# Moving the chunk operators of a state-space layer to VectorE in short steps, pairing the attention heads, and resizing the weight buffers

## The chip, the cores and the metric

The kernel runs on one core of a Trainium2 chip. The metric is the time of one execution in microseconds (us) on the device. A core has five engines that run their own instruction streams in order and wait for one another through semaphores: TensorE (PE in the rows; its weight loads are PEld), VectorE (DVE), ScalarE (ACT), GpSimd (POOL) and SyncE (SP), which here issues nearly all transfers.

## The reference

Two decoder layers over 256 positions of 1024 channels, all in float32. Each layer runs three token mixers on the same input, sums them through gates, projects, and ends with a feed-forward block:

```
for l in range(2):
    z_sgu, z_ssm, q, k, v, gates = split(x @ w_in[l])        # 6144 columns
    br_a = u * (tril(w_s) @ layer_norm(gelu(v_)) + b_s)      # spatial gating
    h[s] = lam_bar * h[s-1] + b_bar @ z_ssm[s]               # complex state, 32 groups x 64
    br_b = glu(gelu(real(c @ h) + d * z_ssm))
    br_c = causal softmax attention, 8 heads of 64, ALiBi    # one block at this length
    merged = sum of sigmoid(gate) * (branch @ w_branch)
    x = layer_norm(alpha * x + merged @ w_out)
    x = layer_norm(alpha * x + (silu(x @ w1) * (x @ w3)) @ w2)
```

## The kernel before, in words

**Weights.** All weights of both layers come as 272 pieces of 128x1024 floats (512 KB), 136 a layer, in the order in which TensorE uses them (`PLAN`). A piece is loaded by SP into one of `RAW` = 4 raw buffers. ScalarE then copies it, rounded, to `whi` (line 103) and VectorE writes the rest, `wlo = raw - whi` (line 104). `whi` and `wlo` have `NSP` = 6 buffers each; a piece's buffers come free when TensorE has finished with it. Every product with weights is three matmuls (hi x hi, hi x lo, lo x hi), recorded by one helper, line 332. The split of piece i+4 is written into the program just ahead of the matmuls of piece i (`LOOK` = 4), and the load of a piece stands behind the split that frees its raw buffer. So VectorE must get through one `wlo` a piece, whatever else it does.

**Order.** `Flow` counts pieces: its position goes up by one with each piece. Code hands it functions with a due position (`at`, `after`), and they are written into the program at the first tick at or past it. That fixes the order on each engine; what runs when is left to the semaphores. Positions below count from the layer's start, if nothing else is said.

**Chunk operators.** The state-space layer works on chunks of 8 positions and needs, for each layer, operators built from its parameters by `ssm_prep`: tables of powers (`tables`, lines 525 to 571), `bbar` (552 to 556), eight `b_chunk` (`bct`, six 128x256 operations each, lines 577 to 581, then four 128x128 transposes on TensorE, `btp`, line 600, and a copy to `bch`), four `c_chunk` (`cchr`, `cchi`, six 128x512 operations each, the same lines 577 to 581), and the response `kch` (line 621): 16 groups of four small products, 16 and 112 columns wide, for two parts. It goes through DRAM (`kd`) and comes back as eight loads into `tch`. For layer 0 this runs inside the layer's own mixers, for layer 1 inside the feed-forward block of layer 0. `b_chunk` and `bbar` run on GpSimd; `c_chunk` runs on VectorE for layer 0 and on GpSimd for layer 1. `bct` has two buffers, so a chunk waits for the transposes of the second last one. The operators are used by `s_in` (`psi`), `y_own` and `y_past` (`pyc`), which begin at position 32 in layer 0 and 16.5 in layer 1 (`SSM_AT`).

**Attention.** For each head, at a step of 1.85 pieces: `att_s` (scores, `pss`, two matmuls over 64 partitions), `att_max` and `att_norm` (VectorE and ScalarE), `att_t` (three transposes, `ppt`) and `att_v` (`pvy`, two matmuls, 64 columns of output partitions). Two heads share one column block of `qT` and `kT`, one in partitions 0 to 63, the other in 64 to 127.

## Time and profile before

| | us |
|---|---|
| three runs, median (lowest to highest) | 921.89 (918.61 to 924.88) |
| the profiled execution | 922.41 |
| its span, first to last instruction | 920.7 |
| TensorE busy in the span | 874.4 |
| VectorE / ScalarE / GpSimd busy | 601.7 / 423.3 / 202.0 |

The profile is of one execution. Matmuls are pipelined, so that one lasts longer than the time to the next; a busy TensorE is therefore not one at its peak, and what a stretch costs is best seen by laying it beside the same stretch of the other layer. The two layers run the same matmuls with weights; what differs is the work around them. The product `pu` opens the second group of weight pieces; it starts at 20.5 us in layer 0 and at 504.3 us in layer 1. The long run of `p` matmuls that ends the first half of the feed-forward block starts at 284.4 and 735.3 us, and its last `f` matmul ends at 483.3 and 909.6 us. These six times cut the span into stretches that can be compared.

### The profile page before, as it was taken

What the parts mean: (1) busy time and instruction counts of PE and PEld (TensorE: products, weight loads), DVE (VectorE), ACT (ScalarE), POOL (GpSimd) and SP (SyncE); (2) the same over time, 40 slices, a digit from 0 to 9 for tenths busy, and PEclk for the clock granted to TensorE, in tenths of its full rate; (3) what the DMA queues carried; (4) which work ended last, traced back from release to release, by engine and by line L of the source; (5) the groups of instructions that cost most, each with busy time, mean ns of one, the idle gap of its engine ahead of it and who ended that gap; (6) DMA issues with size and microseconds to landing.
All of it is one profiled execution on the core that took longest, in us unless ns stands there. A gap on an engine that the chain in (4) does not pass through costs nothing.

```text
span 920.7 us, 14381 instructions
## 1 busy us (share of the span) xinstructions
PE 874.4 (95%) x5665; PEld 751.2 (82%) x5665; DVE 601.7 (65%) x837; ACT 423.3 (46%) x602; POOL 202.0 (22%) x214
## 2 busy tenths in 40 slices
PE   8978899999999989999988999999999999999996
PEld 7877677778878979998976888777888799999995
DVE  7999955755776586677457477545556766555555
ACT  5535355464544425452324463656454254444440
POOL 2349720011200146799000020000112100000002
PEclk9979899999999999999998999999999999999998
DMA  7563347375455717555865664543846466555531
GB/s 284 198 179 120 115 141 173 111 254 186 164 209 177 274 63 255 164 164 179 157 181 172 220 211 130 161 149 126 268 147 226 159 233 221 187 184 186 191 127 46
DMA packets 52803, 163.26 MB, mean 177 GB/s; under 512 B 6240, under 2 KB 11872, under 8 KB 52704
## 3 DMA queue, kind: packets, MB, share of 16 engines
q1 hardware_dynamic: 52592, 162.09, 55.0%
q8 instruction: 44, 0.72, 0.3%
q10 hardware_dynamic: 144, 0.26, 0.1%
q14 instruction: 23, 0.19, 0.1%
HBM read 157.61 MB, written 4.72 MB: 176 GB/s over the span
## 4 chain that ended last, share of the span: by engine, by line
PE 67%; DVE 12%; POOL 8%; issue 6%; DMA 4%; ACT 3%; SPq 0%; POOLq 0%; DVEq 0%; ACTq 0%
PE pw L332 18%; PE pg L332 13%; PE f L332 9%; PE pb L332 5%; DVE wlo L104 4%; DMA raw<-in_wts_dram 3%; PE p L332 3%; PE pbb L332 2%; PE pkq L332 2%; PE po L332 2%; ACT whi L103 2%; PE pv L332 1%; PE pglu L332 1%; POOL tm L580 1%; PE pa L332 1%
## 5 line engine op out<-in xcount | busy, mean ns | idle before, releaser
L104 DVE TENSOR_TENSOR wlo<-raw,whi 128x1024 fp32r<-128x1024 f32 (+1 forms) x273 | 349.7, 1291 | 233.0 <-ACT whi L103 230.5
L103 ACT ACTIVATE whi<-raw 128x1024 fp32r<-128x1024 f32 (+1 forms) x273 | 284.7, 1053 | 218.1 <-PE pw L332 66.8
L332 PE MATMUL pw<-xT,whi 128*128 128x256 f32 x1152 | 207.8, 284 | 0.0
L332 PEld LDWEIGHTS pw<-xT,whi 128*128 128x128 f32 x1152 | 179.9, 191 | 1.6 <-issue 0.2
L332 PE MATMUL pw<-xT,wlo 128*128 128x256 f32 x576 | 163.4, 284 | 4.5 <-DVE wlo L104 4.3
L332 PE MATMUL pg<-whi,xT 128*128 128x512 f32 x384 | 124.8, 407 | 4.3 <-DVE sgm L936 4.3
L332 PEld LDWEIGHTS pw<-xT,wlo 128*128 128x128 f32 x576 | 111.8, 194 | 4.9 <-DVE wlo L104 4.9
L332 PEld LDWEIGHTS pg<-whi,xT 128*128 128x128 f32 x384 | 70.2, 191 | 22.2 <-DVE sgm L936 4.7
L428 POOL TENSOR_SCALAR ve<-mv 128x1 f32<-128x1 f32 x12 | 6.7, 561 | 338.6 <-DVE mv L426 338.5
L1058 POOL TENSOR_TENSOR mg<-mg,tg 128x512 f32<-128x512 f32 x16 | 23.6, 1482 | 248.1 <-DVE tg L1056 248.0
L332 PE MATMUL pg<-wlo,xT 128*128 128x512 f32 x192 | 76.2, 397 | 0.0
L332 PE MATMUL f<-whi,hch 128*128 128x512 f32 x144 | 57.9, 402 | 2.0 <-ACT hch L499 2.0
L332 PE MATMUL f<-whi,hcl 128*128 128x512 f32 x144 | 57.9, 402 | 0.8 <-DVE hcl L500 0.8
L332 PE MATMUL f<-wlo,hch 128*128 128x512 f32 x144 | 56.8, 394 | 0.0
L332 PE MATMUL pkq<-xT,whi 128*128 128x256 f32 x256 | 47.2, 287 | 0.0
L332 PE MATMUL p<-whi,xT 128*128 128x512 f32 x128 | 40.8, 397 | 3.2 <-DVE xT L195 3.2
L332 PEld LDWEIGHTS pg<-wlo,xT 128*128 128x128 f32 x192 | 36.6, 191 | 8.4
L332 PEld LDWEIGHTS pkq<-xT,whi 128*128 128x128 f32 x256 | 39.7, 192 | 1.2 <-issue 1.2
L332 PE MATMUL po<-whi,xT 128*128 128x512 f32 x128 | 40.2, 395 | 0.0
L332 PE MATMUL pkq<-xT,wlo 128*128 128x256 f32 x128 | 36.0, 282 | 0.0
L332 PEld LDWEIGHTS f<-whi,hch 128*128 128x128 f32 x144 | 27.5, 191 | 8.1 <-ACT hch L499 2.4
L332 PEld LDWEIGHTS f<-wlo,hch 128*128 128x128 f32 x144 | 28.0, 194 | 6.4
(265 smaller groups left out, 1522.9 us busy)
## 6 DMA issues: line engine op xcount, KB each, us to landing
raw<-in_wts_dram SPq DMA_DIRECT2D x271, 512.0 KB, 4.0
ln<-in_lng_dram SPq DMA_DIRECT2D x8, 512.0 KB, 8.0
xt<-in_xt_dram SPq DMA_DIRECT2D x4, 256.0 KB, 5.5
ud<-ut SPq DMA_DIRECT2D x4, 256.0 KB, 4.7
xch<-ud SPq DMA_DIRECT2D x8, 128.0 KB, 3.7
zd<-zs SPq DMA_DIRECT2D x8, 128.0 KB, 3.8
ztk<-zd SPq DMA_DIRECT2D x4, 256.0 KB, 4.8
xres<-in_x_dram SPq DMA_DIRECT2D x2, 512.0 KB, 6.9
```

The costliest lines, as they stand in the source:

```text
L103: nc.scalar.activation(hi[:, p], t[:, p], AF.Copy)
L104: nc.vector.tensor_tensor(lo[:, p], t[:, p], hi[:, p].bitcast(F32), OP.subtract)
L332: T_.matmul(o, l, r, start=start, stop=stop, skip_group_check=True)
L428: G.tensor_scalar(ve, mv[:, 1:2], eps, None, OP.add)
L580: lambda: (eng.tensor_tensor(tm, x_re, y_im, OP.mult), eng.tensor_tensor(o_im, o_im, tm, OP.subtract if conj else OP.add))]
L1058: G.tensor_tensor(merged[t][:, cc], merged[t][:, cc], tg, OP.add)
```

## The change

The numbers of the plan: `RAW` 4 to 3 (raw buffers), `NSP` 6 to 7 (split buffers), `SSM_AT` (32, 16.5) to (38, 17), `ATT_STEP` 1.85 a head to 3.75 a pair. A table `SHIFT` of 32 entries moves single steps by -1.5 to +2 pieces. `bbar`, `b_chunk` and `c_chunk` all run on VectorE, in both layers; the six operations of a chunk are handed out in three steps of two, a third of the chunk's step apart, where `b_chunk` was one block before; and the frame tables are spread at 1.25 pieces a step. For layer 0, `c_chunk` comes first (from 12.5, every 2.25), then `b_chunk` (from 22, every 1.6; transposes 3 later). For layer 1, counted from the middle of the feed-forward block, `c_chunk` comes from 8 every 3 and `b_chunk` from 22 every 3. The first 16 columns of `cch` hold the scaled `c`, so that the response is one 128-column product for each group and part. The eight loads of `tch` stand 1.5 pieces apart for layer 1 (1.0 before) and begin at 25 (46 before). One addition of the spatial gating's layer norm moves from GpSimd to VectorE, two small scalings go from VectorE to ScalarE, `as` and `at` have two buffers where they had three, and the last products of layer 0's feed-forward block take both halves in turn for the second row tile.

```diff
-SSM_AT = (32.0, 16.5)
-W2_STEP = (3, 2, 2, 2, 2, 2, 2, 2, 1)
-RAW, NSP, LOOK = 4, 6, 4
+SSM_AT = (38.0, 17.0)
+W2_STEP = (3, 2, 2, 2, 2, 2, 2, 1, 2)
+RAW, NSP, LOOK = 3, 7, 4
-ATT_AT, ATT_STEP = 24.5, 1.85
+ATT_AT, ATT_STEP = 24.5, 3.75
+ASB = 2
...
         def b_chunk(c):
...
-            for f in cmul(G, o[0], o[1], x[0], x[1], y[0], y[1], tm, False):
-                f()
-            st["bct", c] = o
+            for n, f in enumerate(cmul(o[0], o[1], x[0], x[1], y[0], y[1], tm, False)):
+                after(db / 3 * n, f)
...
-            for n, f in enumerate(cmul(E, o[0], o[1], x[0], x[1], y[0], y[1], tm, True)):
+            for n, f in enumerate(cmul(o[0], o[1], x[0], x[1], y[0], y[1], tm, True)):
                 after(dc / 3 * n, f)
...
-                    for part in range(2):
-                        r = cch[k][:, n, 0:112] if part else cst[:, k, n, :]
-                        oo = o[:, 16:128] if part else o[:, 0:16]
-                        T_.matmul(oo, st["bb"][:, k, n, :], r, start=j == 0 and k == 0 and part == 0,
-                                  stop=k == 1, skip_group_check=True, tile_position=(0, 32 * g))
+                    T_.matmul(o, st["bb"][:, k, n, :], cch[k][:, n, 0:P], start=j == 0 and k == 0, stop=k == 1,
+                              skip_group_check=True, tile_position=(0, 32 * g))
...
+        at(t0 - 1.5, scale_c, "scc")
+        for n, f in enumerate(tables()):
+            at(t0 + 0.25 * n, f, "lam")
+        for n, f in enumerate(frame()):
+            at(tb + 1.25 * n, f, f"tab{n}")
+        for c in range(4):
+            at(c0 + dc * c, lambda c=c: c_chunk(c), f"cc{c}")
...
+            at(b0 + db * c, lambda c=c: b_chunk(c), f"bc{c}")
+            at(b0 + db * c + lag, lambda c=c: b_transpose(c), f"bt{c}")
...
-    ssm_prep(0, lambda t, f: fl.at(t, f), V, 8.0, 2.25, 4.25, 6.0, 3.0, 0.75)
+    ssm_prep(0, lambda t, f: fl.at(t, f), 10.5, 24.0, 12.5, 2.25, 22.0, 1.6, 3.0, 0.75)
...
+        def att_s(m):
+
+            bs = [bank("pss") for _ in range(2)]
+            for cs, t in ((slice(0, 128), 0), (slice(128, 384), 1)):
+                for o in range(2):
+                    rr = slice(64 * o, 64 * o + 64)
+                    T_.matmul(bs[o][0][:, cs], qT[rr, m, P * t:P * t + P], kT[rr, m, 0:P * (t + 1)], start=True,
+                              stop=True, skip_group_check=True, tile_position=(64 * o, 0))
...
+            for cs, t, c0 in ((slice(0, 256), 0, 0), (slice(256, 384), 1, 128)):
+                for o in range(2):
+                    h = 2 * m + o
+                    T_.matmul(po[64 * o:64 * o + 64, c0:256], vt[t][:, 64 * h:64 * h + 64], at_s[h][:, cs],
+                              start=t == 0, stop=t == 1, skip_group_check=True, tile_position=(0, 64 * o))
...
-            after(6.0, lambda: ssm_prep(l + 1, lambda t, f: fl.at(pos0 + t, f), G, 8.0, 2.75, 5.25, 24.0, 2.5, 1.0))
+            after(2.0, lambda: ssm_prep(l + 1, lambda t, f: fl.at(pos0 + t, f), 6.0, 8.0, 8.0, 3.0, 22.0, 3.0, 4.5, 1.5))
```

How the order moves, at three places. In brackets stand the semaphores that a row waits for, by the engine or transfer queue that raises them. The first is VectorE in layer 0, before the change, ahead of the split of piece 13. Between the splits of pieces 12 and 13 stand 23 operations of the tables in one block, of which these are the last eleven (`tab` and `tm` are the frame tables and their scratch):

```order
L528 TENSOR_TENSOR lam<-lam,tm 128x16x4
L569 COPY tab<-par_c_138 128x16
L569 COPY tab<-par_s_139 128x16
L525 TENSOR_TENSOR tm<-tab 128x32 [waits DVE_49]
L526 TENSOR_TENSOR tab<-tab 128x32
L527 TENSOR_TENSOR tab<-tab,tm 128x16 [waits DVE_49]
L528 TENSOR_TENSOR tab<-tab,tm 128x16
L525 TENSOR_TENSOR tm<-tab 128x64 [waits DVE_49]
L526 TENSOR_TENSOR tab<-tab 128x32x2
L527 TENSOR_TENSOR tab<-tab,tm 128x16x2 [waits DVE_49]
L528 TENSOR_TENSOR tab<-tab,tm 128x16x2
L104 TENSOR_TENSOR wlo_514<-raw_390,whi_513 128x1024 [waits DMAHW5_49,PE_49,Activation_49]
```

With the change the tables stand elsewhere, and a typical place of the busiest stretch of layer 0 on VectorE reads so (`tmb` is the scratch of `b_chunk`, `ISA` the score step of attention, each `wlo` a piece):

```order
L107 TENSOR_TENSOR wlo_1116<-raw_952,whi_1115 128x1024 [waits DMAHW6_49,PE_49,Activation_49]
L584 COPY tab<-par_c_136 128x16
L593 TENSOR_TENSOR bct<-bct,tmb 128x256 [waits DVE_49]
L594 TENSOR_TENSOR bct<-bu,lam 128x256
L107 TENSOR_TENSOR wlo_1147<-raw_998,whi_1146 128x1024 [waits DMAHW7_49,PE_49,Activation_49]
L595 TENSOR_TENSOR tmb<-bu,lam 128x256 [waits DVE_49]
L596 TENSOR_TENSOR bct<-bct,tmb 128x256 [waits DVE_49]
L1003 ISA as,ast<-pss,dist 128x128 [waits PE_49]
L1003 ISA ast 128x1
L1003 ISA as,ast<-pss,dist 128x256
L1003 ISA ast 128x1
L592 TENSOR_TENSOR bct<-bu,lam 128x256 [waits PE_49]
```

What moved: a chunk's six operations stand in twos between the splits, beside the attention's. The last of these rows opens a `b_chunk` and waits for TensorE. The second place is GpSimd before the change, where that wait stood: a whole `b_chunk` of layer 0 and the addition behind it.

```order
L577 TENSOR_TENSOR bct<-bu,lam 128x256 [waits PE_49]
L577 TENSOR_TENSOR tm<-bu,lam 128x256 [waits Activation_49]
L578 TENSOR_TENSOR bct<-bct,tm 128x256 [waits Pool_49]
L579 TENSOR_TENSOR bct<-bu,lam 128x256
L580 TENSOR_TENSOR tm<-bu,lam 128x256 [waits Pool_49]
L581 TENSOR_TENSOR bct<-bct,tm 128x256 [waits Pool_49]
L916 TENSOR_TENSOR vv<-vv,sg_b 128x512 [waits DMAHW3_49,DVE_49]
```

What moved: the six operations and their wait for TensorE went from GpSimd's queue to VectorE's, where the next pieces' `wlo` stand behind them. The third place is TensorE in layer 0 where the scores of a head are made, before the change (`pg`, the gates' products, around them):

```order
L332 MATMUL pg_1170<-whi_982,xT 128x512 x2
L332 MATMUL pg_1170<-wlo_983,xT 128x512
L973 MATMUL pss<-kT,qT 128x128
L974 MATMUL pss<-kT,qT 128x256
L332 MATMUL pg_1182<-whi_982,xT 128x512 x2
L332 MATMUL pg_1182<-wlo_983,xT 128x512
L332 MATMUL pg_1182<-whi_982,xT 128x512 x2
```

and with the change (here the products of a branch, `pb`, stand around them):

```order
L614 MATMUL btp<-ident,bct 128x128 x4
L992 MATMUL pss<-kT,qT 128x128 x2
L992 MATMUL pss<-kT,qT 128x256 x2
L1020 MATMUL ppt<-ident,as 128x128 x3
L340 MATMUL pb_1298<-whi_1115,brah 128x512
L340 MATMUL pb_1298<-whi_1115,bral 128x512
L340 MATMUL pb_1298<-wlo_1116,brah 128x512
```

What moved: two heads' score products stand side by side, as do, later, two heads' `pvy` products (64x256 twice, then 64x128 twice).

## Rows read from the trace of the kernel before

**Rows 1.** The page: busy time, share of the span and instructions of each engine, and the granted clock in 40 slices of the span (9 is full speed).

```profile
PE 874.4 (95%) x5665; PEld 751.2 (82%) x5665; DVE 601.7 (65%) x837; ACT 423.3 (46%) x602; POOL 202.0 (22%) x214
PEclk9979899999999999999998999999999999999998
```

**Rows 2.** Windows: the stretch and its length, then busy time of PE, PEld, DVE, ACT and POOL with instruction counts, granted clock, DMA share and GB/s. The first two rows are layer 0 from `pu` to the feed-forward block, the next two the same in layer 1, then the feed-forward block of layer 0 and of layer 1.

```profile
20.50:140.00 119.50, 103.19 (x688) 89.38 (x687) 102.38 (x190) 55.59 (x92) 62.33 (x66) 0.91 0.48 152
140.00:284.40 144.40, 141.85 (x888) 111.11 (x887) 92.70 (x131) 69.90 (x114) 14.00 (x12) 1.00 0.56 179
504.30:618.00 113.70, 111.84 (x869) 92.51 (x867) 67.84 (x105) 61.89 (x108) 6.12 (x11) 1.00 0.54 175
618.00:735.30 117.30, 114.84 (x547) 92.46 (x546) 72.84 (x91) 56.04 (x82) 14.95 (x12) 1.00 0.56 185
284.40:483.30 198.90, 189.37 (x1348) 174.01 (x1347) 128.87 (x144) 83.09 (x98) 91.75 (x81) 0.97 0.60 182
735.30:909.60 174.30, 174.30 (x1186) 161.22 (x1185) 97.88 (x100) 75.22 (x83) 0.84 (x3) 1.00 0.54 178
```

**Rows 3.** Timeline of TensorE: two neighbouring groups of the response; each group ends with the four records of a `cst` row.

```profile
432.86 0.24 PE L621 MATMUL kch<-cst,bb 128*32 128x16 f32 x4
...
433.15 0.24 PE L621 MATMUL kch<-cst,bb 128*32 128x16 f32 x4
```

**Rows 4.** Groups of TensorE over the whole span: 128-column products on four column groups of 32, and full-array transposes of 128 columns.

```profile
L780 PE MATMUL psi<-bch,uch 128*32 128x128 f32 x128 | 4.5, 276 | 1.9 <-ACT uch L762 1.9
L485 PE MATMUL mtp<-ident,mg 128*128 128x128 f32 x32 | 4.5, 272 | 0.0
```

**Rows 5.** Waits of TensorE: what waited, for what, us in total, times, longest.

```profile
PE psu L332 <- DVE wlo L104: 5.9, 2, 3.5
PE pw L332 <- DVE wlo L104: 4.3, 1, 4.3
PE pg L332 <- DVE sgm L936: 4.3, 1, 4.3
PE btp L600 <- POOL bct L581: 4.1, 2, 2.9
PE kch L621 <- POOL cchi L581: 2.2, 1, 2.2
```

**Rows 6.** Timeline of VectorE in layer 0: start, us, line, operation. Left out between the `wlo` rows are the tables.

```profile
39.95 1.22 DVE L104 TENSOR_TENSOR wlo<-raw,whi 128x1024 fp32r<-128x1024 f32 x1 [1.17 <-ACT whi L103]
...
47.70 1.64 DVE L104 TENSOR_TENSOR wlo<-raw,whi 128x1024 fp32r<-128x1024 f32 x1
...
55.99 3.49 DVE L104 TENSOR_TENSOR wlo<-raw,whi 128x1024 fp32r<-128x1024 f32 x3
```

**Rows 7.** Groups of VectorE from 740 to 900 us (layer 1, feed-forward): busy us, mean ns of one.

```profile
L104 DVE TENSOR_TENSOR wlo<-raw,whi 128x1024 fp32r<-128x1024 f32 x59 | 72.3, 1225 | 65.7 <-ACT whi L103 65.1
```

**Rows 8.** Windows of 20 us in the mixers of layer 0, same columns.

```profile
40.00:60.00 20.00, 14.12 (x81) 13.10 (x80) 19.48 (x43) 6.17 (x8) 8.88 (x12) 0.79 0.55 165
100.00:120.00 20.00, 16.01 (x166) 13.09 (x166) 19.86 (x23) 5.56 (x9) 14.67 (x13) 0.83 0.35 112
```

**Rows 9.** Groups of VectorE from 360 to 437 us (layer 0, feed-forward).

```profile
L104 DVE TENSOR_TENSOR wlo<-raw,whi 128x1024 fp32r<-128x1024 f32 x25 | 42.4, 1711 | 17.4 <-ACT whi L103 17.4
L500 DVE SCALAR_TENSOR_TENSOR hcl<-hh,hch 128x512 fp32r<-128x512 f32 x4 | 5.3, 1328 | 0.0
```

**Rows 10.** Groups of VectorE from 70 to 120 us (layer 0, mixers).

```profile
L104 DVE TENSOR_TENSOR wlo<-raw,whi 128x1024 fp32r<-128x1024 f32 x11 | 18.0, 1633 | 1.6 <-ACT whi L103 1.6
L580 DVE TENSOR_TENSOR tm<-cst,lam 128x512 f32<-128x512 f32 x4 | 4.5, 1129 | 0.0
```

**Rows 11.** Groups of VectorE over the whole span: two-input operations of the two sizes at issue, where GpSimd is idle.

```profile
L812 DVE TENSOR_TENSOR vch<-rot 128x256 f32<-128x256 f32 x4 | 1.7, 426 | 0.1
L455 DVE TENSOR_TENSOR xres<-xres,ln 128x512 f32<-128x512 f32 x2 | 1.3, 680 | 0.0
```

**Rows 12.** Transfers over the whole span: size, median us from issue to landing.

```profile
raw<-in_wts_dram SPq DMA_DIRECT2D x271, 512.0 KB, 4.0
tch<-kd SPq DMA_DIRECT2D x2, 256.0 KB, 7.1
```

**Rows 13.** Transfers from 436 to 490 us (layer 0's `tch` loads for layer 1 and its last pieces).

```profile
raw<-in_wts_dram SPq DMA_DIRECT2D x14, 512.0 KB, 6.7
```

**Rows 14.** Groups of GpSimd over the whole span.

```profile
L579 POOL TENSOR_TENSOR bct<-bu,lam 128x256 f32<-128x256 f32 x16 | 17.7, 1109 | 0.0
L577 POOL TENSOR_TENSOR bct<-bu,lam 128x256 f32<-128x256 f32 x16 | 13.7, 857 | 32.0 <-PE btp L600 19.2 <-DVE lam L527 6.7 <-DVE lam L528 6.1
```

**Rows 15.** Timeline of TensorE in layer 1: the scores of one head up to its first transposes, and the value products of one head.

```profile
588.28 0.48 PE L973 MATMUL pss<-kT,qT 64*128 64x128 f32 x2
588.61 0.59 PE L974 MATMUL pss<-kT,qT 64*128 64x256 f32 x2
589.13 0.55 PE L1000 MATMUL ppt<-ident,as 128*128 128x128 f32 x3
593.77 0.65 PE L1014 MATMUL pvy<-at,vt 128*64 128x256 f32 x2
594.26 0.38 PE L1016 MATMUL pvy<-at,vt 128*64 128x128 f32 x2
```

**Rows 16.** The page: the group of ScalarE that makes `whi`, over the whole span (busy us, mean ns of one, idle time before them and what ended it).

```profile
L103 ACT ACTIVATE whi<-raw 128x1024 fp32r<-128x1024 f32 (+1 forms) x273 | 284.7, 1053 | 218.1 <-PE pw L332 66.8
```

More of the change, by code (lines that the diff above doesn't have):

```diff
@@ L168, in tile_hybrid_trunk @@
     tick, after = fl.tick, fl.after
-    prs = sp.tile([P, 56 * DEPTH], F32, tag="as", name="prs", bufs=3)
+    prs = sp.tile([P, 56 * DEPTH], F32, tag="as", name="prs", bufs=ASB)
     xT = cp.tile([P, 2, KD, S], F32R, name="xT")
@@ L358, in go @@
             if q == npc - 1:
-                after(ev[t] if isinstance(ev, (tuple, list)) else ev, lambda: evac(t, *outs[t]))
+                after((ev[t] if isinstance(ev, (tuple, list)) else ev) + SHIFT.get(f"{fl.layer}e{name}", 0),
+                      lambda: evac(t, *outs[t]))
             if t == 1:
@@ L639, in response_load, with at @@
                               k_dram.rearrange("h (g m) -> h g m", g=8)[:, :, 0:4 * P - 64 * t])
[L641 to L652 removed]
+        def at(t, f, key):
+            put(t + SHIFT.get(str(l) + key, 0), f)
+        at(t0 - 1.5, scale_c, "scc")
[5 more added lines that the diff above has]
+            at(c0 + dc * c, lambda c=c: c_chunk(c), f"cc{c}")
+        for c in range(2):
+            at(c0 + dc * c + 0.5 * dc, lambda c=c: bbar(c), f"bb{c}")
+        for c in range(8):
+            at(b0 + db * c, lambda c=c: b_chunk(c), f"bc{c}")
+            at(b0 + db * c + lag, lambda c=c: b_transpose(c), f"bt{c}")
+        t1 = c0 + 4 * dc + 1.5
+        at(t1, response, "resp")
         for t in range(LC):
[L654 removed]
+            at(t1 + 3.5 + lt * t, lambda t=t: response_load(t), "rl")
     dram = ctx.enter_context(tc.tile_pool(name="dram", bufs=1, space=bass.MemoryType.DRAM))
@@ L668, in tile_hybrid_trunk @@
     bch = cp.tile([P, 16, 2, P], F32, name="bch")
-    cch = [cp.tile([P, 16, P], F32, name="cch" + s) for s in "ri"]
+    cch = [cp.tile([P, 16, P + 16], F32, name="cch" + s) for s in "ri"]
     tch = cp.tile([P, 8, 4 * P], F32, name="tch")
@@ L696, in tile_hybrid_trunk, with at @@
         fl.pos = base
-        def at(t, f):
-            fl.at(base + t, f)
+        fl.layer = l
+        def at(t, f, key=""):
+            fl.at(base + t + SHIFT.get(str(l) + key, 0), f)
         sg = {}
@@ L1239, in tile_hybrid_trunk @@
         for t in range(2):
-            for c in range(2):
-                for n, kk in enumerate(range(done, FFT)):
-                    w2_part(kk, t, c, last[n])
-                    if t == c == 1:
-                        W.finish()
-                    tick(0.25)
-                after(0.25, lambda t=t, c=c: (ln_half(t, c, a2[t, c][0]), a2[t, c][1]()))
+            order = [(c, n) for c in range(2) for n in range(FFT - done)]
+            if t == 1 and not end:
+                order = [(c, n) for n in range(FFT - done) for c in range(2)]
+            for c, n in order:
+                w2_part(done + n, t, c, last[n])
+                if t == c == 1:
+                    W.finish()
+                tick(0.25)
+                if n == FFT - done - 1:
+                    after(0.25, lambda t=t, c=c: (ln_half(t, c, a2[t, c][0]), a2[t, c][1]()))
             after(0.25, lambda t=t: ln_last(t, gb2) if end else ln_fin(t, gb2, keep))
```

194 lines of the change are left out of this document (89 added, 105 removed).

## The prediction

> **What bounds the kernel now.** I read the page first: TensorE is busy for 874.4 of 920.7 us, VectorE for 601.7, and the granted clock drops only here and there [rows 1]. A TensorE that is busy for 95% looks like the end of the matter, but matmuls overlap, so busy time says little. I therefore laid the two layers side by side, since their weight matmuls are the same [rows 2]. From the product `pu` to the same point of the feed-forward block, layer 0 takes 119.5 + 144.4 = 263.9 us and layer 1 takes 113.7 + 117.3 = 231.0: 32.9 more. The rest of the feed-forward block takes 198.9 and 174.3: 24.6 more. These 57.5 us are what the operators of both layers cost, since both are built in layer 0's time, one set in each stretch. TensorE's own share is small: a response is 16 groups of 433.15 - 432.86 = 0.29 us [rows 3], 4.6 us, and 32 transposes at 4.5 / 32 = 0.14 us [rows 4] are 4.5 us at most, together 9.1 in each stretch. So 57.5 - 18.2 = 39.3 us are waits and half clock: about 23.8 in the mixers, 15.5 in the feed-forward block.
>
> The waits name the cause [rows 5]: TensorE waited for `wlo` of VectorE, for `sgm` of VectorE, and for `bct` and `cchi` of GpSimd. Two things make VectorE late. First, blocks: between two splits stands the whole frame table, and the splits begin at 39.95, 47.70 and 55.99 us [rows 6], where a piece goes by in 2.7 us (59 splits in 160 us [rows 7]). In that window TensorE is busy for 14.12 of 20 us and the granted clock averages 0.79 of the full 2.4 GHz, that is, part of it at 1.2 [rows 8]. Second, GpSimd: a split takes 1.225 us where GpSimd is idle [rows 7], 1.711 beside its chunk operators in the feed-forward block [rows 9] and 1.633 in the mixers [rows 10].
>
> **The change, part by part.** The sum is made against the profiled execution, 922.4 us (span 920.7 and 1.7 around it), which stands 0.5 above the median of 921.89.
>
> *Chunk operators on VectorE.* A 128x256 operation with two inputs takes 0.426 us there, a 128x512 one 0.680 [rows 11]. Layer 0's mixers get 48 operations of `b_chunk` and 6 of `bbar` at 0.426, 23.0 us, and 2 additions of 0.68, 1.4: 24.4 in. What leaves: its 24 `c_chunk` operations took about 1.13 beside GpSimd [rows 10] and will take 0.68, 10.8 us; about 20 splits that stood beside GpSimd's 62.3 busy us lose 0.41 each, 8.2 us [rows 2, 7, 10]. That is 24.4 - 19.0 = 5.4 us more for VectorE, which was busy for 102.4 of 119.5 us in the first stretch [rows 2]. So VectorE is not relieved, it is smoothed: TensorE's inputs no longer queue behind a block of 23 operations, and the chunks are spread as far as position 36. If VectorE were busy without a pause, the first stretch could end at 102.4 + 5.4 = 107.8 us, 11.7 earlier. That is the upper bound of this term in the first stretch, 0 is the lower one, and I take 10, since the blocks go for certain. The state-space products move from position 32 to 38, out of the crowded stretch into one in which TensorE was busy for 141.85 of 144.4 us, so they cost there what they save here; I count neither.
>
> In the feed-forward block VectorE gets 24 `c_chunk` operations (16.3 us) and the same 54 smaller ones (23.0), and loses 25 x 0.49 = 12.2 of slow splits and 4 x 0.64 = 2.6 of slow `hcl` (1.328 against a `128x512` operation of 0.68) [rows 7, 9, 11]: 128.9 + 24.5 = 153.4 of 198.9 us [rows 2]. It has room. The waits for GpSimd go, and the loads of `tch` move away from the layer's end, where raw loads took 6.7 us to land instead of 4.0 [rows 12, 13]. Of 15.5 us I take 13; bounds 4 (the wait for `wlo` of 4.3 alone) and 15.5. The cover is 3 to 4 pieces of split weights ahead of TensorE, some 8 to 11 us. If it is gone, each late operation shows in full.
>
> *The wait that moves.* GpSimd waited 19.2 us for TensorE's `btp` ahead of `bct` [rows 14]; that wait now stands on VectorE, with the next splits, evacuations and attention steps behind it. The old wait was long because GpSimd ran ahead. VectorE is as loaded as TensorE and will mostly arrive later. I price it at 0 and keep 9.6 us (half of it, the part that the four pieces ahead may not cover) for the rivals.
>
> *Attention in pairs.* One head's scores last from 588.28 to 589.13, 0.85 us; its value products some 0.73 (0.49 to the second shape's start, and half as much for half the columns) [rows 15]. Sixteen heads: 25.3 us. Two heads side by side use different rows of the array for scores, different columns for values. If they overlap fully, half goes: 12.6 us; if not, 0. The nearest row is `psi`: 128 products on neighbouring column groups are busy for 4.5 us in all, 0.035 each, where full-array passes of the same 128 columns take 0.14 [rows 4]. So neighbours in different groups do overlap, by more than two. I take 10.5 of 12.6, as some of layer 0's attention lies where VectorE, not TensorE, ends last.
>
> A rule speaks against the half of this that uses columns: the Trainium skill, "TensorE: Matmul & The Clock Gate", section "Part 3: Packing small matmuls — row/col tiling", says that a weight load overlaps running matmuls only when its row group differs. The two heads' value products share all rows; by that rule half of their 11.7 us, 5.8, would not go and the sum would be up to 5 us higher, about 893. The `psi` products share all rows too, and 0.035 us each leaves no room for weight loads that stand alone, so this case's trace does not agree.
>
> *Half the response products.* 0.29 us a group holds two 16-column and two 112-column products; without the former I estimate 0.23 (0 to 0.29 as bounds): 32 x 0.06 = 2 us.
>
> *Buffers.* A raw buffer is taken while its load lands and is split: 4.0 + 1.05 (`whi`) + 1.2 = 6.3 us [rows 7, 12, 16]. Three of them give a piece every 2.1 us, against 2.7 needed; four gave 1.6. I price it at 0; where a load takes 6.7 us [rows 13], it is 9.0 / 3 = 3.0, and the pieces ahead must cover the difference, so I give up 1 us for the `tch` loads. The seventh split buffer may help where pieces are held longer, at the layer's seam; no row prices that, so 0.
>
> Sum: 10 + 13 + 10.5 + 2 - 1 = 34.5; 922.4 - 34.5 = 887.9, say **888 us**.
>
> **Rivals.**
> *VectorE inherits the wait.* VectorE arrives at `bct` first, waits for transposes, and the splits behind it come late. For it: both engines are near full in layer 0, the pieces are coupled both ways, and `btp` in turn must find its chunk ready. Against it: VectorE is the busier one. The smoothing in the mixers then brings nothing and the feed-forward block gives up 4: 888 + 10 + 4 = 902; with the whole 9.6 instead, 912.
> *The pairs don't overlap.* Then 10.5 stays: 898. For it: no row shows two 64-row groups beside each other. Against it: `psi`.
> *All waits go.* 23.8 + 15.5 + 12.6 + 2 = 53.9: 868. Against it: VectorE's 107.8 us above.
> *Slower: three raw buffers starve the split.* With three, a load that takes over 3 x 2.7 - 2.3 = 5.8 us makes weights the bound. Transfers of `tch` took 7.1 [rows 12], raw loads beside them 6.7. If raw loads take 8 us for 80 of the 272 pieces, each costs (8 + 2.3) / 3 - 2.7 = 0.73, 59 us: 888 + 59 = 947 less the 10 that the pieces ahead cover, 937. Against it: the median of 4.0 over 271 loads, and three quarters of the span have no `tch` load near.
> *The change doesn't do what it says* on VectorE if short steps still pile up, since a tick hands out all that is due; that is the first rival again.
>
> **How the numbers follow.** The forecast's own case (878 to 897) has 0.49, VectorE's wait 0.20, no overlap 0.13, all waits gone 0.10, starved splits 0.08. About 1% is what a measurement of this kernel tells from no change: 912.7 and 931.1. The first, third and fourth case lie below 912.7, and so does most of the second: 0.49 + 0.13 + 0.10 + 0.09 = 0.81 faster. The rest of the second is 0.11 for the same, 0.08 slower. The range from 867 to 911 leaves out the starved case and the end of the second and fourth.
>
> **What would show it.** In the profile after: splits at 1.23 us everywhere; GpSimd busy well under 100 us; no wait of TensorE for GpSimd; the stretch from `pu` to the feed-forward block some 15 us shorter in layer 0 and 5 in layer 1; the feed-forward block of layer 0 within 15 us of layer 1's; scores and values of a pair in about the time of one head. Wrong would be: VectorE's waits for `btp` or TensorE's for `wlo` over 10 us in all, `pss` and `pvy` as long as before, or ScalarE's `whi` waiting for raw loads ahead of TensorE's waits.

## The result and the profile after

The changed kernel takes 881.29 us (median of four runs, 877.84 to 881.99), the kernel before 922.32 in the same job: a ratio of 0.9551, 95% interval 0.9509 to 0.9592. The forecast of 888 was 6.7 us too high, within its range. The profiled execution after took 881.44 us, its span 879.7. The page, against [rows 1]:

```profile
PE 840.5 (96%) x5537; PEld 727.3 (83%) x5537; DVE 613.2 (70%) x971; ACT 423.5 (48%) x604; POOL 54.2 (6%) x78
PEclk9989989999999999999999999999999999999998
```

GpSimd's busy time fell from 202.0 to 54.2 us, VectorE's rose by only 11.5 although it took over the chunks. The four stretches between the same matmuls as in [rows 2] (from `pu` to the feed-forward block in layer 0 and in layer 1, then the two feed-forward blocks; start, end and length, busy PE, PEld, DVE, ACT and POOL, granted clock, DMA share, GB/s):

```profile
20.40:271.80 251.40, 233.09 (x1511) 191.77 (x1509) 195.06 (x379) 128.03 (x210) 22.74 (x23) 0.97 0.56 176
473.60:695.20 221.60, 218.74 (x1414) 181.46 (x1412) 144.04 (x198) 118.58 (x192) 17.27 (x21) 1.00 0.57 185
271.80:452.90 181.10, 178.83 (x1283) 165.24 (x1283) 140.83 (x221) 84.05 (x99) 1.33 (x2) 1.00 0.70 202
695.20:868.60 173.40, 173.40 (x1185) 161.06 (x1185) 95.31 (x98) 74.34 (x82) 0.79 (x2) 1.00 0.56 182
```

Layer 0's mixers took 263.9 us and take 251.4, layer 1's 231.0 and now 221.6, layer 0's feed-forward block 198.9 and now 181.1, layer 1's 174.3 and now 173.4. The largest part came from the feed-forward block: it stands 7.7 us behind layer 1's, where it stood 24.6 behind (the mark of its last `f` product stands 2.2 us, in layer 1 2.7, ahead of that product's end, in both kernels alike). Layer 0's mixers are still 29.8 behind layer 1's (32.9 before).

A part of this is TensorE's clock. The same windows from layer 0's mark to the next `pu`, before and after:

```profile
284.40:504.30 219.90, 207.59 (x1421) 188.47 (x1420) 146.16 (x165) 91.89 (x109) 93.08 (x83) 0.95 0.59 180
271.80:473.60 201.80, 196.10 (x1357) 178.74 (x1357) 156.87 (x242) 90.82 (x108) 2.70 (x4) 0.99 0.68 198
```

In the trace the time at 1.2 GHz adds up to 20.5 us in the first row and to 3.4 in the second; the rest is at 2.4 GHz. In layer 0's mixers it is 17.1 where it was 20.5. Before, each fall of the clock in this stretch came with a stop of TensorE, of 4.3, 2.2, 2.0 and 2.5 us, or just behind it; after, a stop of 2.3 us for a chunk had none behind it. At the lower level a 512-column product took 0.43 us to the next one, at 2.4 GHz 0.23 (`f` from 475.43 and from 479.14 us), so a wait with a fall behind it costs more than its own length. The 17.1 us less at the lower level are worth at most some 8 of this stretch's 18.1; that is an estimate from these rows.

The groups of VectorE over the whole span that answer to [rows 7, 9, 10, 11] (busy us, mean ns of one, idle time ahead and what ended it):

```profile
L107 DVE TENSOR_TENSOR wlo<-raw,whi 128x1024 fp32r<-128x1024 f32 (+1 forms) x273 | 334.6, 1233 | 182.8 <-ACT whi L106 180.0 <-PE f L340 1.3
L509 DVE SCALAR_TENSOR_TENSOR hcl<-hh,hch 128x512 fp32r<-128x512 f32 x18 | 12.3, 685 | 2.0 <-ACT hch L508 2.0
L592 DVE TENSOR_TENSOR bct<-bu,lam 128x256 f32<-128x256 f32 x16 | 6.7, 419 | 0.0
L595 DVE TENSOR_TENSOR tmc<-cchr,lam 128x512 f32<-128x512 f32 x8 | 5.5, 685 | 0.0
```

A split takes 1.233 us on average over the whole span now, the operations of a chunk 0.42 and 0.68, as the prediction costed them. TensorE's waits, against [rows 5] (total, times, longest):

```profile
PE utp L778 <- ACT xgr L770: 4.6, 1, 4.6
PE btp L614 <- DVE bct L596: 3.9, 3, 2.3
PE ppt L1020 <- ACT bch L615: 3.4, 1, 3.4
PE kch L632 <- DVE cchi L596: 2.1, 1, 2.1
```

The long waits for `wlo` and `sgm`, 14.5 us in all, are gone. The waits for chunks are not: they moved with the chunks to VectorE, 3.9 and 2.1 us where 4.1 and 2.2 stood. New are two waits for ScalarE, 8.0 us: `utp` (transposes of the state-space input, which wait for its reordered copy `xgr`) and `ppt`. Among VectorE's waits no row names `btp` (0.5 us in the second profile, `a_same` below): it did not inherit the 19.2 us that GpSimd had waited [rows 14].

### The profile page after: what moved, and what is told of

Its sections match the earlier page's. It is cut to its first block, busy times and chain, and to the rows that moved or that the text cites. A ratio compares the mean times of both kernels' runs of the same rounds, so it can differ in the third digit from the quotient of the medians.

```text
span 879.7 us, 14083 instructions
## 1 busy us (share of the span) xinstructions
PE 840.5 (96%) x5537; PEld 727.3 (83%) x5537; DVE 613.2 (70%) x971; ACT 423.5 (48%) x604; POOL 54.2 (6%) x78
## 4 chain that ended last, share of the span: by engine, by line
PE 54%; DVE 18%; issue 10%; DMA 9%; ACT 6%; POOL 2%; SPq 1%; POOLq 0%; DVEq 0%; ACTq 0%
PE pw L340 15%; PE pg L340 13%; PE f L340 9%; DMA raw<-in_wts_dram 8%; DVE wlo L107 7%; PE pb L340 4%; ACT whi L106 3%; PE p L340 2%; PE pkq L340 2%; PE pbb L340 2%; PE pglu L340 1%; PE pu L340 1%; DMA ud<-ut 1%; POOL mg L1075 1%; PE pyc L855 1%
## 5 line engine op out<-in xcount | busy, mean ns | idle before, releaser
L107 DVE TENSOR_TENSOR wlo<-raw,whi 128x1024 fp32r<-128x1024 f32 (+1 forms) x273 | 334.6, 1233 | 182.8 <-ACT whi L106 180.0
L106 ACT ACTIVATE whi<-raw 128x1024 fp32r<-128x1024 f32 (+1 forms) x273 | 285.5, 1053 | 230.1 <-DMA raw<-in_wts_dram 153.8
L340 PE MATMUL pw<-xT,whi 128*128 128x256 f32 x1152 | 203.7, 280 | 0.0
L340 PEld LDWEIGHTS pw<-xT,whi 128*128 128x128 f32 x1152 | 176.5, 188 | 1.6 <-issue 0.2
L340 PE MATMUL pw<-xT,wlo 128*128 128x256 f32 x576 | 161.2, 280 | 0.0
L340 PE MATMUL pg<-whi,xT 128*128 128x512 f32 x384 | 122.4, 400 | 0.0
L340 PEld LDWEIGHTS pw<-xT,wlo 128*128 128x128 f32 x576 | 109.8, 191 | 0.1
L340 PE MATMUL f<-whi,hcl 128*128 128x512 f32 x144 | 56.1, 389 | 0.0
L340 PEld LDWEIGHTS f<-whi,hcl 128*128 128x128 f32 x144 | 27.1, 188 | 5.0
```

The lines of the kernel that those rows point to most:

```text
L106: nc.scalar.activation(hi[:, p], t[:, p], AF.Copy)
L107: nc.vector.tensor_tensor(lo[:, p], t[:, p], hi[:, p].bitcast(F32), OP.subtract)
L340: T_.matmul(o, l, r, start=start, stop=stop, skip_group_check=True)
```

## The experiments

Each was timed in five rounds beside the kernel before; since the runs were made in groups on different chips, ratios to it are compared. `a_same` ran in one group with `b_pairs`, `a_block` and `a_raw46`. The stretches are those of the windows above, from each run's own profile; the third reaches here to the next `pu`.

| run | median us | ratio to before (95%) | mixers 0 | mixers 1 | feed-forward 0 to `pu` |
|---|---|---|---|---|---|
| before | | 1 | 263.9 | 231.0 | 219.9 |
| after | 881.29 | 0.9551 (0.9509 to 0.9592) | 251.4 | 221.6 | 201.8 |
| after again, `a_same` | 879.32 | 0.9537 (0.9507 to 0.9568) | 249.9 | 222.1 | 199.7 |
| `b_pairs` | 915.84 | 0.9930 (0.9902 to 0.9957) | 268.0 | 224.9 | 215.9 |
| `b_frame` | 912.04 | 0.9903 (0.9875 to 0.9932) | 261.1 | 230.7 | 214.6 |
| `a_single` | 878.35 | 0.9545 (0.9521 to 0.9569) | 250.2 | 221.8 | 199.9 |
| `a_resp2` | 880.39 | 0.9561 (0.9540 to 0.9582) | 249.3 | 222.5 | 201.9 |
| `a_block` | 885.54 | 0.9596 (0.9568 to 0.9625) | 255.2 | 221.8 | 202.9 |
| `a_bpool0` | 875.29 | 0.9503 (0.9481 to 0.9524) | 247.8 | 221.6 | 199.4 |
| `a_bpool1` | 882.50 | 0.9580 (0.9555 to 0.9605) | 249.9 | 221.5 | 204.8 |
| `a_pool1` | 889.19 | 0.9646 (0.9621 to 0.9671) | 250.2 | 221.8 | 208.3 |
| `a_late` | 884.31 | 0.9606 (0.9580 to 0.9633) | 251.2 | 222.0 | 204.0 |
| `a_raw46` | 878.34 | 0.9521 (0.9492 to 0.9551) | 249.0 | 222.2 | 199.7 |
| `a_best` | 877.10 | 0.9520 (0.9495 to 0.9546) | 248.1 | 221.5 | 200.8 |

**The changed kernel again** (`a_same`), no edit:

> The kernel after, unchanged, to have its time beside the other runs of this group on one chip and to see how far two profiles of the same program differ. Every theory: 878 to 882 us.

It took 879.32 us. Two profiles of this one program differ by 1.5 us in layer 0's mixers and 2.1 in its feed-forward block: that is the grain of the table, and a difference of 2 us in a stretch says nothing yet.

**Attention in pairs alone** (`b_pairs`), on the kernel before; the functions `att_s` and `att_v` and their steps are those of the diff, buffers as before (the load of `x` for the residual moves 1.7 pieces earlier with them):

```diff
-ATT_AT, ATT_STEP = 24.5, 1.85
+ATT_AT, ATT_STEP = 24.5, 3.75
-        def att_s(h):
+        def att_s(m):
...
-        def att_v(h):
+        def att_v(m):
```

> The kernel before, with the attention in pairs of heads alone. Theory of the prediction (two heads' products overlap, and most of TensorE's time in them counts): 10 to 13 us faster, 909 to 912. Rival (in layer 0 the attention lies where VectorE and ScalarE end last, so only layer 1's half counts): 6 us faster, 916, the mixers of layer 1 shorter by 6 and those of layer 0 the same.

The ratio is 0.9930, some 6.5 us. The windows of the two mixers, layer 0 and layer 1:

```profile
20.40:288.40 268.00, 241.32 (x1575) 199.35 (x1574) 195.82 (x321) 125.50 (x206) 76.66 (x78) 0.94 0.53 165
504.30:729.20 224.90, 220.74 (x1415) 183.25 (x1414) 140.53 (x195) 117.83 (x191) 21.02 (x23) 0.99 0.58 185
```

Layer 1 gains 6.1 of the 6.3 us that half of 12.6 makes: there the pairs overlap fully and count fully. Layer 0 gains nothing, its mixers are 4.1 longer. That is the rival's side, which had them unchanged: TensorE's time in the attention does not set the end there. The granted clock of that stretch is 0.94, where it was 0.96 [rows 2], that is 30.7 us at 1.2 GHz instead of 20.5, and TensorE has new waits in it (`ppt` 3.8 us, `pg` 3.1). That two heads at once make a longer block for VectorE and ScalarE, and so bring these waits, is my reading. In the feed-forward block another 4.0 went, where this edit changes no instruction; that is twice the grain. It goes with 10.2 us at 1.2 GHz instead of 20.5; why TensorE stopped less there is open. What the pairs do in layer 0 of the changed kernel, where the steps around them differ, no run shows.

**Head after head** (`a_single`), on the changed kernel:

```diff
-            for cs, t in ((slice(0, 128), 0), (slice(128, 384), 1)):
-                for o in range(2):
+            for o in range(2):
+                for cs, t in ((slice(0, 128), 0), (slice(128, 384), 1)):
...
-            for cs, t, c0 in ((slice(0, 256), 0, 0), (slice(256, 384), 1, 128)):
-                for o in range(2):
+            for o in range(2):
+                for cs, t, c0 in ((slice(0, 256), 0, 0), (slice(256, 384), 1, 128)):
```

> The kernel after, with one change: the score and value products of a pair are written head after head (first both of one head, then both of the other) instead of alternately; placement on the array and everything else stay. Theory (products overlap only where neighbours stand in different row or column groups): of four products in a row only the middle two are then neighbours in different groups, so about two thirds of the 12.9 us that TensorE's time for pss and pvy fell by come back, +8 us, about 889. Rival (the gain came from fewer, larger steps and not from the overlap): within 2 us of 881.

No difference. My reason for the forecast of +8 fell, and so did the rival's reason, since the overlap stayed. TensorE's timeline around the scores of a pair, first as changed, then head after head:

```profile
567.57 0.39 PE L340 MATMUL pg<-wlo,xT 128*128 128x512 f32 x1
567.88 0.93 PE L992 MATMUL pss<-kT,qT 64*128 64x128 f32 x8
568.74 0.50 PE L340 MATMUL pg<-whi,xT 128*128 128x512 f32 x1
```

```profile
564.80 0.39 PE L340 MATMUL pg<-wlo,xT 128*128 128x512 f32 x1
565.12 0.93 PE L992 MATMUL pss<-kT,qT 64*128 64x128 f32 x8
565.98 0.50 PE L340 MATMUL pg<-whi,xT 128*128 128x512 f32 x1
```

A pair's scores take 0.86 us to the next product in both, where one head alone took 0.85 [rows 15]. The single records of the scores head after head say how (start in us and columns; each product has two records):

```
565.118  128
565.131  128
565.331  128
565.344  128
565.443  256
565.456  256
565.661  256
565.674  256
```

The order in the kernel's text is 128, 256, 128, 256 columns, and still the two 128-column products start 13 ns apart and both 256-column ones come after them. The second head's first product started ahead of the first head's second; the instructions of the built program were not listed for this run, so whether TensorE or the build changed the order is not shown. Here it was enough that products for different parts of the array stood near each other; they did not have to alternate. The value products of a pair, which differ in columns of the array alone:

```profile
576.52 0.87 PE L1032 MATMUL pvy<-at,vt 128*64 128x256 f32 x8
577.32 0.50 PE L340 MATMUL pb<-whi,brah 128*128 128x512 f32 x1
```

They take 0.80 us for two heads, where one took about 0.73 [rows 15]. The rule of the Trainium skill that spoke against it ("TensorE: Matmul & The Clock Gate", section "Part 3: Packing small matmuls — row/col tiling", a weight load overlaps running products only when its row group differs) does not agree with this trace: these products use all 128 rows, and the saving is nearly as full as for the scores.

**The response in two products again** (`a_resp2`):

```diff
-                    T_.matmul(o, st["bb"][:, k, n, :], cch[k][:, n, 0:P], start=j == 0 and k == 0, stop=k == 1,
-                              skip_group_check=True, tile_position=(0, 32 * g))
+                    for c0, c1 in ((0, 16), (16, P)):
+                        T_.matmul(o[:, c0:c1], st["bb"][:, k, n, :], cch[k][:, n, c0:c1],
+                                  start=j == 0 and k == 0 and c0 == 0, stop=k == 1,
+                                  skip_group_check=True, tile_position=(0, 32 * g))
```

> The kernel after, with one change: each 128-column product of the response is written as a 16-column and a 112-column product again. Theory (a 16-column product costs TensorE as much time as the 36 ns that the records of before show, so that halving the products was worth 5 us and not the 2 of the prediction): +4 to +5.5 us, about 886. Rival (the prediction's size): +2 us, 883.

It took 880.39, ratio 0.9561, within the interval of the unchanged kernel and nearer the rival's 2 us. TensorE's own time for the response did change. In the changed kernel, layer 1's response (16 groups, four to each pair of rows; the first rows and the last, with the product behind):

```profile
346.20 0.45 PE L632 MATMUL kch<-cchr,bb 128*32 128x128 f32 x8
346.44 0.42 PE L632 MATMUL kch<-cchi,bb 128*32 128x128 f32 x8
...
347.75 0.49 PE L632 MATMUL kch<-cchi,bb 128*32 128x128 f32 x8
348.17 0.38 PE L340 MATMUL pw<-xT,whi 128*128 128x256 f32 x1
```

It lasts from 346.20 to 348.17, 0.12 us a group where it was 0.29 [rows 3]. That is 2.7 us a layer, 5.4 in all, more than the 2 of the prediction; but the kernel's time shows at most 2 of it. One reason stands in the traces: layer 0's response lasts 4.90 us in `a_resp2` and still 4.39 in the changed kernel, since the quicker one stops for 2.1 us to wait for `cchi`.

**Chunks in one block** (`a_block`), both kinds, both layers:

```diff
             for n, f in enumerate(cmul(o[0], o[1], x[0], x[1], y[0], y[1], tm, False)):
-                after(db / 3 * n, f)
+                f()
...
             for n, f in enumerate(cmul(o[0], o[1], x[0], x[1], y[0], y[1], tm, True)):
-                after(dc / 3 * n, f)
+                f()
```

> The kernel after, with the six operations of each chunk (b and c, both layers) written as one block at the chunk's first step instead of in three steps. Theory of the prediction (short steps let the splits through, which is what the mixers of layer 0 gain from): 5 to 10 us slower, 884 to 891. Rival (a block of six lasts 2 to 4 us, and the three to four pieces ahead cover it): within 2 us of the unchanged kernel.

It is 6 us slower than `a_same` in the same job (885.54 against 879.32), and the mixers of layer 0 took most of it: 255.2 against 249.9; the feed-forward block took 3.2 more, little above the grain. The short steps are worth about 5 us in layer 0's mixers. The same work on the same engine, in other places between the splits, costs that much.

**Frame tables spread alone** (`b_frame`), on the kernel before:

```diff
-            at(t0 + 0.125 * n if n < 14 else t0 + 3.0 + 0.5 * n, f)
+            at(t0 + 0.125 * n if n < 5 else t0 + 14.0 + 1.25 * (n - 5), f)
...
-            u = tm[:, :n * 2 * k].rearrange("p (c i t) -> p c i t", i=n, c=2)
+            t = work("gq", (P, 512), name="tmt", bufs=3) if tm is None else tm
+            u = t[:, :n * 2 * k].rearrange("p (c i t) -> p c i t", i=n, c=2)
...
-            todo += doubling(V, tabv, tm, 16, NCH)
+            todo += doubling(V, tabv, None, 16, NCH)
```

> The kernel before, with the frame tables alone spread (their eight steps from piece 22 on, 1.25 apart, in place of 0.125 apart from piece 8.6 on). Theory of the prediction (the block of 23 operations between two splits is one of two causes of what layer 0's mixers lose): 4 to 8 us faster, 914 to 918, the wait of psu for wlo gone. Rival (the block is paid later, where VectorE is as full): within 2 us of 922.

912.04 us, ratio 0.9903, 8 to 9 us faster than before and more than the 4 to 8 expected: a fifth of the change by moving eight steps (with a scratch tile for each step in place of one for all). The waits of TensorE that are left at the head of its list:

```profile
PE pg L332 <- DVE sgm L937: 4.5, 1, 4.5
PE btp L601 <- POOL bct L582: 4.4, 4, 2.1
```

The wait of `psu` for `wlo` is no longer there, as forecast. But the mixers of layer 0 fell by 2.8 only, and the feed-forward block, where layer 1's tables lie, by 5.3. The trace of the kernel before shows what stood there. Two splits of VectorE stand with the tables ahead of them and between them, and TensorE waits for the second, its longest wait of that block; in `b_frame` that wait is gone:

```profile
333.74 1.69 DVE L104 TENSOR_TENSOR wlo<-raw,whi 128x1024 fp32r<-128x1024 f32 x1
341.62 2.35 DVE L104 TENSOR_TENSOR wlo<-raw,whi 128x1024 fp32r<-128x1024 f32 x2
```

```profile
342.89 0.58 PE L332 MATMUL pw<-xT,wlo 128*128 128x256 f32 x1 [4.31 <-DVE wlo L104]
```

**Layer 1's chunks back on GpSimd**, the b chunks alone (`a_bpool1`) and all of them (`a_pool1`), at the steps of the changed kernel. The diff is that of `a_pool1`; `a_bpool1` has the first two of its three places, and `a_bpool0` the same with layer 0 in place of 1. `bbar` stays on VectorE in all of them:

```diff
-        def cmul(o_re, o_im, x_re, x_im, y_re, y_im, tm, conj):
+        def cmul(o_re, o_im, x_re, x_im, y_re, y_im, tm, conj, V=V):
...
-            for n, f in enumerate(cmul(o[0], o[1], x[0], x[1], y[0], y[1], tm, False)):
+            for n, f in enumerate(cmul(o[0], o[1], x[0], x[1], y[0], y[1], tm, False, G if l in (1,) else V)):
...
-            for n, f in enumerate(cmul(o[0], o[1], x[0], x[1], y[0], y[1], tm, True)):
+            for n, f in enumerate(cmul(o[0], o[1], x[0], x[1], y[0], y[1], tm, True, G if l in (1,) else V)):
```

> The kernel after, with one change: the six operations of each b_chunk of layer 1 (made in layer 0's feed-forward block) run on GpSimd, at the same steps; layer 0's stay on VectorE. Theory (GpSimd beside the splits and the waits for it were the 15 us that this stretch lost): the stretch of the feed-forward block grows by 5 to 12 us, 886 to 893. Rival (the waits went because the steps are spread and come earlier, whichever engine does them): within 3 us of 881.

> The kernel after, with all of layer 1's chunks (b and c) on GpSimd, as before the change, but at the steps of the changed kernel. Theory of the prediction (the 15 us of the feed-forward block went because GpSimd no longer stands beside the splits): that block 8 to 12 us longer than in the unchanged kernel, 888 to 892. Rival (what went there was mostly the place and spread of the work and of its loads, not the engine): 2 to 5 us longer, 881 to 885, as with the b chunks alone.

The b chunks alone cost 5.1 us in that stretch against `a_same` and 3.0 against the first profile, and the interval of their ratio overlaps that of the unchanged kernel, so that they cost something is likely and not sure. All chunks cost 8.6 and 6.5 (208.3 against 199.7 and 201.8), and the whole time with them rises to 889.19, its interval clear of both. Groups of VectorE and GpSimd from 300 to 445 us with all of them on GpSimd, then VectorE's splits in the same stretch of the changed kernel:

```profile
L107 DVE TENSOR_TENSOR wlo<-raw,whi 128x1024 fp32r<-128x1024 f32 x48 | 67.8, 1417 | 33.2 <-ACT whi L106 32.9
L596 POOL TENSOR_TENSOR bct<-bct,tmb 128x256 f32<-128x256 f32 x8 | 9.4, 1171 | 0.6
L592 POOL TENSOR_TENSOR bct<-bu,lam 128x256 f32<-128x256 f32 x8 | 8.6, 1070 | 21.3 <-PE btp L614 21.3
```

```profile
L107 DVE TENSOR_TENSOR wlo<-raw,whi 128x1024 fp32r<-128x1024 f32 x51 | 62.2, 1222 | 23.7 <-ACT whi L106 23.4
```

A split takes 1.417 us on average with them and 1.222 without, and GpSimd needs 1.07 to 1.17 us for an operation that VectorE does in 0.42. VectorE as a whole is hardly busier with the chunks than without: 156.8 us in that stretch (`a_same`) against 152.8, though it does 72 operations more. TensorE's cost comes mostly in one place: it waits 4.5 us for a `wlo`, and the stretch has 10.2 us at 1.2 GHz instead of 3.4. So the engine is worth some 7 to 9 us of that stretch's 18 to 20.

> The kernel after, with one change: the six operations of each b_chunk of layer 0 run on GpSimd, at the same steps; layer 1's stay on VectorE. Theory of the prediction (VectorE gains in layer 0's mixers because its splits no longer stand beside GpSimd): splits at 1.6 us in that stretch, +3 to +8 us, 884 to 889. Rival (in layer 0's mixers the end is set by the chain between VectorE's and ScalarE's queues, in which the 48 operations are links, so they are better elsewhere): 2 to 6 us faster, 875 to 879.

875.29, ratio 0.9503: not slower, as my theory had it, but faster or the same. The splits did not go to 1.6 us either: from 85 to 150 us they average 1.307, against 1.221 in the changed kernel. Layer 0's mixers are at 247.8, 2.1 below `a_same`. The intervals (0.9481 to 0.9524, 0.9507 to 0.9568) overlap, so it is not settled that GpSimd is the better place there; but no gain from the b chunks' move to VectorE is to be seen in layer 0. VectorE's busy time tells why so little hangs on it: 48 operations of 0.42 us, 20 us in all, left it, and it was busy for 188.4 us in place of 195.6, since what stayed ran slower.

**Late `tch` loads** (`a_late`):

```diff
-            at(t1 + 3.5 + lt * t, lambda t=t: response_load(t), "rl")
+            at(t1 + 3.5 + lt * t if l == 0 else 46.0 + t, lambda t=t: response_load(t), "rl")
```

> The kernel after, with layer 1's eight tch loads issued from piece 46 of the feed-forward block, one a piece, as before the change, in place of from 25, one in one and a half. Theory (the loads at the layer's end, close together, held the raw loads up): the feed-forward block 4 to 6 us longer, 883 to 886. Rival (hidden either way): within 1.5 us of the unchanged kernel.

4.3 us more up to the next `pu` (204.0 against 199.7, and 2.2 against the first profile), and a ratio of 0.9606, above the intervals of both runs of the unchanged kernel (its own interval overlaps the wider of them). So the early loads are worth some 2 to 6 us. They do not land sooner for it (up to 13.6 us each in the changed kernel, 13.9 here), but there they meet other work than at the layer's end; which of its transfers the late ones hold up was not taken apart.

**Buffers of before** (`a_raw46`):

```diff
-RAW, NSP, LOOK = 3, 7, 4
+RAW, NSP, LOOK = 4, 6, 4
```

> The kernel after, with the buffers of before: four raw and six split buffers. Theory of the prediction (both are worth nothing apart from 1 us): within 1.5 us of the unchanged kernel. Rival (in the mixers of layer 0 ScalarE waited 16 us for raw loads, so the third raw buffer is missed): 3 to 6 us faster. Second rival (the seventh split buffer carries the pieces over the stalls of layer 0): 3 to 6 us slower.

878.34 against 879.32: no difference. Three raw buffers cost no time, and the seventh split buffer gave none, or the two cancel: they were changed together. What three raw buffers did change is what ScalarE's `whi` waits for: raw loads for 153.8 us over the span in the changed kernel and 36.2 here (34.9 in the kernel before).

**Both small gains together** (`a_best`), the edits of `a_bpool0` and `a_raw46`:

> The kernel after, with layer 0's b chunks on GpSimd and four raw and six split buffers. If both small gains seen alone are real and add: 872 to 875. If they were the spread between runs of one program: 877 to 880.

877.10, ratio 0.9520. The two do not add; they lie within the spread between runs. No version here is surely better than the changed kernel.

## Why the prediction held, step by step

**Smoothing in layer 0's mixers (10 us).** The stretch fell by 12.5, and not in the way that the step said. Undoing the short steps gives back 5, the spread tables gave 2.8 in the kernel before, and the pairs alone cost 4 there. What did not count is the engine: with the b chunks back on GpSimd the stretch is not longer than with them on VectorE. The parts that were not tried apart (c chunks first, products of the state space later, single shifts, the pairs beside the new steps) hold the rest, some 8 us, and its cause is open. Nor was the sum for VectorE right in its terms: the 24 `c_chunk` operations averaged 1.05 us before and not 1.13, since [rows 10] shows the slowest of their groups, and the splits from 20 to 150 us averaged 1.374, 32 of them, which is some 5 us to lose and not 8.2. The tables' operations were not in it; they took 10.4 us before and take 6.2. In all, VectorE was busy for 195.1 us of the mixers before and after, where 5.4 more was expected. VectorE did not come near "busy without a pause": 102.4 of the first 119.5 us were the bound, but the stretch ends where VectorE and ScalarE wait for each other. In the changed kernel, 105 to 113 us, first ScalarE, then VectorE (start, us; in brackets the idle time before and what ended it):

```profile
105.47 0.40 ACT L1007 ACTIVATE as<-as,ast 128x128 f32<-128x128 f32 x1 [4.56 <-DVE ast L1003]
...
106.37 1.04 ACT L106 ACTIVATE whi<-raw 128x1024 fp32r<-128x1024 f32 x1
109.59 0.40 ACT L1007 ACTIVATE as<-as,ast 128x128 f32<-128x128 f32 x1 [2.17 <-DVE ast L1003]
```

```profile
106.38 0.18 DVE L584 COPY tab<-par_s 128x16 f32<-128x16 f32 x1
107.45 1.22 DVE L107 TENSOR_TENSOR wlo<-raw,whi 128x1024 fp32r<-128x1024 f32 x1 [0.90 <-ACT whi L106]
...
109.26 0.28 DVE L1003 CUSTOM_DVE_ANT_0 as<-pss,dist 128x128 f32<-128x128 f32 x1
...
111.57 0.42 DVE L592 TENSOR_TENSOR tmb<-bu,lam 128x256 f32<-128x256 f32 x1
112.72 1.22 DVE L107 TENSOR_TENSOR wlo<-raw,whi 128x1024 fp32r<-128x1024 f32 x1 [0.73 <-ACT whi L106]
```

ScalarE stands 4.56 us for the row maximum of a head (`ast`), and `whi` of the next piece is queued behind it; VectorE then waits 0.90 us for that `whi`, and the maximum of the next head is queued behind its split and two chunk operations. A piece goes by in 5.27 us here (107.45 to 112.72), with neither engine full. The chain goes on to TensorE. The split from 112.72 has VectorE's `RECIPROCAL` of an attention step behind it, ScalarE's scaling waits for that with `bch` behind it, and TensorE stops for 3.41 us; behind that stop its products stand 0.43 us apart until 120.5:

```profile
113.87 0.16 DVE L1012 RECIPROCAL ast<-ast 128x2 f32<-128x2 f32 x1
```

```profile
114.12 0.80 ACT L1014 ACTIVATE as<-as,ast 128x128 f32<-128x128 f32 x2 [1.43 <-DVE ast L1012]
114.82 0.57 ACT L615 ACTIVATE bch<-btp 128x512 f32<-128x512 f32 x1
```

```profile
115.45 0.90 PE L1020 MATMUL ppt<-ident,as 128*128 128x128 f32 x3 [3.41 <-ACT bch L615]
```

From 100 to 120 us VectorE is busy for 16.5 and ScalarE for 10.6:

```profile
100.00:120.00 20.00, 14.40 (x65) 10.81 (x64) 16.50 (x51) 10.59 (x22) 0.00 (x0) 0.85 0.70 183
```

The same 20 us stand in [rows 8], with other work in them: there VectorE was idle for 0.14 us and was itself the end; now it is idle for 3.5, and TensorE does no more than before, 14.40 us against 16.01. These two queues are one part of what is left of layer 0's 29.8 us; the wait of `utp` for `xgr`, 4.6 us, is another. That the queues set the end here is read from the trace; no run took them apart.

**Feed-forward block (13 us).** The term was too small. From the mark in [rows 2] to the next `pu` the stretch fell by 18.1. GpSimd's part is 8.6 (`a_pool1`), the place of the `tch` loads 4.3 (`a_late`), the frame tables 5.3 (`b_frame`), the shorter response up to 2.7. The first two were taken against `a_same`, where the fall is 20.2. The four make 20.9; with a grain of 2 us in each, that they add up so well is chance. The step named the first two and the upper bound of 15.5 for all waits; what it missed is that the block of tables stood in this stretch too, for layer 1. It was counted in layer 0's mixers alone; the wait of 4.3 us that the step took as its lower bound is the one behind that block. VectorE's busy time up to the last `f` rose by 12.0 us and not by 24.5, so GpSimd had slowed more than the splits and `hcl` that the step counted.

**Attention in pairs (10.5 us).** Mechanism right, place wrong. The overlap is nearly full: eight pairs of 0.86 and 0.80 us take 12.0 less than the 25.3 of before. But in the kernel before only layer 1's half reaches the end (`b_pairs`). The step took off 2 for layer 0; it should have taken off 6, if that holds in the changed kernel too.

**Response (2 us).** TensorE saved 5.4, because the 16-column products cost more than the estimate of a fifth of a group. The kernel's time shows at most 2. The term came out right by luck, of two errors.

**Buffers (-1 us) and the wait for `btp` (0).** The buffers made no difference in `a_raw46`, and no row shows the wait. With that the rivals of the inherited wait and of starved splits fall. One sign that the prediction named as wrong did come, though: ScalarE's `whi` now waits for raw loads first of all, where it had waited for TensorE [rows 16]:

```profile
L106 ACT ACTIVATE whi<-raw 128x1024 fp32r<-128x1024 f32 (+1 forms) x273 | 285.5, 1053 | 230.1 <-DMA raw<-in_wts_dram 153.8 <-PE pw L340 28.0 <-PE f L340 15.4
```

It was no sign of lost time: with four raw buffers these waits go back to 36.2 us and the kernel's time stays. The pieces split ahead must have covered them. The other signs came as forecast, but for 0.4 us in which TensorE still waits for GpSimd (`mtp`). TensorE's waits for `wlo` are 3.8 us in all, under the 10 that would have spoken against the forecast; the layer's first half got 12.5 and 9.4 us shorter in the two layers where it said some 15 and 5, and layer 0's feed-forward block came to within 7.7 us of layer 1's, where it said 15.

In sum the stretches give 12.5 + 9.4 + 18.1 + 0.9 = 40.9 of the span's 41.0: the mixers of both layers 21.9, where the prediction had 10 + 10.5 and half of the response's 2, and the feed-forward block 18.1 where it had 13. That the mixers' sum fits so well is luck: the pairs gave less than forecast, and as much came from causes that were not in the sum. Of layer 1's 9.4, 6.1 are the pairs; for the other 3.3 there is no run.

## What to carry to other kernels

Lay the same matmuls of two layers side by side: the difference is what the extra work costs, whoever is busy; then look which two in-order queues feed each other in that stretch, since TensorE time saved there need not shorten anything (the pairs of layer 0 in `b_pairs`). Spreading a block of small vector operations over the pieces can be worth as much as moving work to another engine: eight steps of tables gave 8 to 9 us alone, all of layer 1's chunks off GpSimd some 7 to 9, and the b chunks of layer 0 on either engine made no sure difference. A stop of TensorE costs more than its length when its clock falls behind it. Where two engines slow each other, count the slow-down of the other's operations as part of the price of the work.

## What the runs showed of the hardware

Products for different row groups ran side by side although another product for the first group was written between them (starts 13 ns apart in `a_single`, the pair in 0.86 us in either order), so not every stream was run in the order of its text. Products for different column groups that share all rows did so too (two heads' values in 0.80 us, one head's in 0.73). With the stops of TensorE in layer 0's feed-forward block before (2.0 to 4.3 us) the granted clock fell to 1.2 GHz, and 512-column products stood 0.43 us apart in place of 0.23. VectorE's splits took 1.417 us on average beside GpSimd's chunks and 1.222 without them (`a_pool1` and the changed kernel, 300 to 445 us). A 16-column product was not cheap: leaving out half of the products took a response group from 0.29 to 0.12 us, though the columns computed stayed the same.
